# Norm rows loaded for every partition, an overflow branch moved into the last quad, and attention's last steps spread over the output projection

## The chip, the cores and the metric

The kernel runs on one core of a Trainium2 chip. The time is that of one execution on the device, in microseconds. Its engines each work through their own queue in order: TensorE (PE, weight loads as PEld), VectorE (DVE), ScalarE (ACT), GpSimd (POOL), and SyncE (SP), which here issues the loads.

## The reference

A trunk of two layers on 256 tokens of width 1024, float32. Each layer is a mixer and a mixture of experts, each followed by a norm of the sum:

```
for i in range(2):
    mix = even_mixer(x) if i == 0 else odd_mixer(x)   # SSD || stick-breaking; MLA || forgetting attention
    x = layer_norm(2**0.5 * x + mix, ln1_g[i], ln1_b[i])
    ffn = hier_moe(x)          # 4 groups x 4 experts, best group, best 2 experts of it
    x = layer_norm(2**0.5 * x + ffn, ln2_g[i], ln2_b[i])
expert e: (silu(t @ w_gate[e]) * (t @ w_up[e])) @ w_down[e], weighted by the token's gate
```

The odd mixer's eight latent-attention heads need low-rank queries (q_up) and keys and values (kv_up), a rotated key part (rope), and its eight forgetting heads a running sum of log sigmoid(f).

## The kernel before

All weights come through a ring of 19 tiles of 128 x 2048 (1 MB each). `ring_init` takes the list of loads in order; `fill` issues the next ones on SP whenever `ring_done` or `gdone` says in the program that a tile is free. SP runs in order, so a load waits until the last reader of the tile it takes is done, and everything behind it waits too. Eight loads can be under way, one per lane. Activations take tiles of the same ring (`G`), after `reserve`.

Weights of the mixers are used as sums of two rounded pieces: `split` (L230, L231) makes them, the high one on ScalarE, the low one on VectorE, `presplit` two steps ahead of TensorE.

An expert layer (`moe`) gathers up to 32 tokens for each of 16 experts, in four quads of four experts, for two halves t of the tokens. For each quad TensorE runs `gate_up` (L1054; eight weight tiles, each for both t), `act` and `turn`, the combination of the quad before, and `down` (L1084; four tiles). Results stand in PSUM: pools of four banks "a" and four "b". `overflow` is a branch in every engine's program, taken only if some expert has over 32 tokens; here it isn't. The engines do not wait for each other at it; but each waits for its own earlier work before it leaves the untaken side (L1274 EVENT_SEMAPHORE), SP for all eight lanes, and tiles that the branch uses come free when the engines that would have read them are past it. It takes all four "b" banks and stands after quad 2's `down`.

The scale and bias of a norm (1 x 2048, `ln`) are loaded into one partition of a ring tile and spread by GpSimd (`ln_rows`, L805, four broadcasts); then `gain_rows` (L812, L813) applies them to `xres`, the residual, on GpSimd. This happens in each expert layer (at quad 2), in `key_rope` of the odd mixer, and in the finale.

The odd mixer (`mixer1`) goes through a list: four value strips, q_up 0 and 1, kv_up, eight strips of q and k. On GpSimd's queue stand, in this order, `key_rope` (emitted at the first strip: clear krep, the norm's row, gain_rows of half 0, rope) and `forget` (from the second strip on). In `forget`, ScalarE takes one exponential (L200) in the middle of GpSimd's steps; in ScalarE's queue it stands ahead of the split of q_up 1's weights. Attention runs one step behind the other in `attention(j)`: scores(j), probs_T(j-1), norm_probs(j), attend(j-2). Its steps 0 to 6 go between the q and k strips, steps 7, 8, 9 after chunks 0, 1, 2 of the output projection (`out_proj`, L707 to L709, eight chunks), which uses the last head pair in chunk 7.

Of the kernel before, what the change touches and what calls it, by code (L numbers as in the profile page):

```python
# [14 lines left out]
AF = mybir.ActivationFunctionType  # L15
# [79 lines left out]
class Builder:  # L95
# [703 lines left out]
    def ln_rows(self, i):  # L799

        self.rows.add(i)
        w = self.ring[i]
        for k in range(4):
            r = w[:, 512 * k:512 * k + 512]
            self.nc.gpsimd.partition_broadcast(r, r[0:1], channels=128)  # L805
        return w.rearrange("p (k n) -> p k n", k=2)

    def gain_rows(self, t, gb, cs=slice(0, 1024)):

# [85 lines left out]
    def moe(self, layer, seq0, mixer, tiles=0):  # L895
# [303 lines left out]
        for q in (1, 2, 3):  # L1199
            if q == 2:  # L1200
                if layer == 0:
                    self.router_prep(1)
                gb = self.ln_rows(seq0 + 24)
                self.gain_rows(1, gb)
                self.gain_rows(0, gb)
            for c in range(4):
                for t in range(2):
                    gate_up(q, t, (c,))
            gate_up(q, 0, range(4, 8))
            act(q, 0)  # L1210
            if q == 1:
                rows_hi(0)
                rows_lo(0)
            gate_up(q, 1, range(4, 8))
            act(q, 1)
            turn(q, 0)
            if layer == 0 and q == 1:
                self.router_load(1)
            both(combine, q - 1, 0)
            if q == 1:  # L1220
                rows_hi(1)
                rows_lo(1)
                gather(0, 1, (1, 3))
            both(combine, q - 1, 1)
            if layer == 0 and q == 2:
                self.router_sums(1)
            turn(q, 1)
            if q == 1:
                gather(1, 1, (1, 3))
                self.gdone(2)  # L1230
            if q == 3:
                sc.preload_act_table_set(EXP_LN)
                break
            both(down, q, 0)
            if q == 2 and self.stop != "noov":
                self.reserve(2)
            both(down, q, 1)
            if q == 2 and self.stop != "noov":
                self.gdone(1)
                self.overflow(layer, [R[t]["gate"] for t in range(2)], [R[t]["ov"] for t in range(2)],  # L1240
                              n_max)
        yield
        both(down, 3, 0)
        combine(3, 0, 0)
# [19 lines left out]
    def overflow(self, layer, gate, ov, n):  # L1264

        nc = self.nc
        v, sc, pe = nc.vector, nc.scalar, nc.tensor
        gu = [self.B("fgu") for _ in range(2)]
        b, o = self.B("fht"), self.B("fo")
        fw = self.G([128, 2, 1024], name="fw")  # L1270
        fw = fw[:, 0], fw[:, 1]
        sg, ht = self.T([128, 256], name="fsg"), self.T([128, 2, 128], name="fhT")
        x1T = self.G([128, 8, 256], name="x1T")
        with self.tc.If(n > 32, label=f"over{layer}") as branch:  # L1274
            for t in range(2):

                v.scalar_tensor_tensor(ov[t], gate[t], 1.0 / ALPHA, ov[t], op0=OP.mult, op1=OP.mult)
                for c in range(8):
                    pe.transpose(b[:, :128], self.xres[:, t, 128 * c:128 * c + 128], self.ident)
                    v.tensor_copy(x1T[:, c, 128 * t:128 * t + 128], b[:, :128])  # L1280
            for e in range(16):
                q, i = divmod(e, 4)
                cs = slice(512 * i, 512 * i + 512)
                for c2 in range(4):
                    k = c2 % 2
                    nc.sync.dma_start(fw[k].rearrange("p (c n) -> p c n", c=2),
                                      self.a["wgu"][layer, q, 2 * c2:2 * c2 + 2, :, cs].rearrange("c p n -> p c n"))
                    w = fw[k].rearrange("p (c n) -> p c n", c=2)
                    for c in range(2):
                        cc = 2 * c2 + c  # L1290
                        for t in range(2):
                            pe.matmul(gu[t], x1T[:, cc, 128 * t:128 * t + 128], w[:, c, :],
                                      start=(cc == 0), stop=(cc == 7))
                for s in range(2):
                    nc.sync.dma_start(fw[s].rearrange("p (k n) -> p k n", k=2),
                                      self.a["wd"][layer, q, 2 * s:2 * s + 2, :, cs].rearrange("c p n -> p c n"))
                for t in range(2):
                    sc.activation(sg, gu[t][:, :256], AF.Silu)
                    v.tensor_mul(sg, sg, gu[t][:, 256:])
                    for k in range(2):  # L1300
                        pe.transpose(b[:, 128 * k:128 * k + 128], sg[:, 128 * k:128 * k + 128], self.ident)
                    v.tensor_copy(ht, b[:, :256].rearrange("p (k n) -> p k n", k=2))
                    for s in range(2):
                        c = slice(512 * s, 512 * s + 512)
                        for k in range(2):
                            pe.matmul(o, ht[:, k, :], fw[s][:, 512 * k:512 * k + 512], start=(k == 0), stop=(k == 1))
                        v.scalar_tensor_tensor(self.xres[:, t, c], o, ov[t][:, e:e + 1], self.xres[:, t, c],
                                               op0=OP.mult, op1=OP.add)
        if layer == 0:
            with branch.Else():  # L1310
                self.hint(1)

        self.gdone(2)
# [30 lines left out]
    def mixer1(self, s0, moe):  # L1344
# [5 lines left out]


        order = [("v", i) for i in range(4)] + [("q", 0), ("q", 1), ("kv", 0)] + [("s", i) for i in range(8)]
        first = {"v": s0 + 2, "q": s0 + 4, "kv": s0 + 5, "s": s0 + 7}

        def presplit(n):
            if n >= len(order) or order[n] in pieces:
# [87 lines left out]

        def key_rope():
            nc.gpsimd.memset(krep[:, :, :64], 0.0)
            gb.append(self.ln_rows(s0 + 6))
            for k in range(4):
                self.gain_rows(0, gb[0], slice(256 * k, 256 * k + 256))
            self.rope(nc.gpsimd, krep[:, :, 64:80], krep[:, :, 80:96], rest[:, :, 128:144], rest[:, :, 144:160],  # L1450
                      self.cv("cosk").rearrange("p (t n) -> p t n", t=2),
                      self.cv("sink").rearrange("p (t n) -> p t n", t=2), [128, 2, 16])
            nc.gpsimd.tensor_copy(krep[:, :, 96:], krep[:, :, 64:96])
# [148 lines left out]

        def attention(j):

            steps = [(scores, 0), (probs_T, 1), (norm_probs, 0), (attend, 2)]
            if j == 7:
                steps.insert(0, steps.pop())
            for f, d in steps:
                if 0 <= j - d < 8:
                    f(*divmod(j - d, 4))  # L1610

# [70 lines left out]
            m = mix[k // 4]  # L1682
            return m[:, k % 4, :], m[:, 4 + k % 4, :]

        yield from self.out_proj(8, LEAD1, wsplit, mixk, 2, 6, after=lambda k: attention(7 + k))


def moe_seq(a, layer):
# [9 lines left out]
def build(ctx, tc, a, out, stop=None):  # L1698
    b = Builder(ctx, tc, a, out, stop)
    seq = [a["w0"][i] for i in range(16)] + [a["wout0"][i] for i in range(6)]  # L1700
    m0 = len(seq)
    seq += moe_seq(a, 0)
    s1 = len(seq)
    seq += [a["wab"][0], a["wab"][1], a["wfv"][0], a["wfv"][1], a["wqu"], a["wkvu"], a["ln"][1]]
    seq += [a["wfox"][i] for i in range(4)]
    seq += [a["wout1"][i] for i in range(4)]
    m1 = len(seq)
    seq += moe_seq(a, 1) + [a["ln"][3]]
    b.ring_init(seq, {m + i for m in (m0, m1) for i in LP})
    if stop is None:  # L1710
        b.hint(0)
    nc = tc.nc
    orow = out.rearrange("(t p) d -> p t d", p=128)

    def dump_acc(gen):
        for acc in gen:
            pass
        for t in range(2):
            for s in range(2):
                nc.vector.tensor_copy(b.xres[:, t, 512 * s:512 * s + 512], acc[t][s])  # L1720
        nc.sync.dma_start(orow, b.xres)

    mix = b.mixer0()
    if stop == "mix0":
        return dump_acc(mix)
    moe = b.moe(0, m0, mix, 2)
    if stop in ("moe0", "noov"):
        return dump_acc(moe)
    mix = b.mixer1(s1, moe)
    if stop == "mix1":  # L1730
        return dump_acc(mix)
    moe = b.moe(1, m1, mix)
    next(moe)
    gb = b.ln_rows(m1 + 49)
    b.finale(gb, orow, moe)


def lay_out(inputs):
# [51 lines left out]
    wr[:, :, 8:24] = inputs["moe_w_expert"]  # L1790
    o["wr"] = f(wr.reshape(2, 8, 128, 32).transpose(0, 2, 1, 3))
    o["pp"] = pp
    o["ln"] = f(np.stack([lng, lnb], 1)).reshape(4, 1, 2048)
    gate = inputs["moe_w_gate"].reshape(2, 4, 4, 8, 128, 256)
    up = inputs["moe_w_up"].reshape(2, 4, 4, 8, 128, 256)

# [22 lines left out]
```

## Time and profile before

| what | value |
|---|---|
| median of 3 runs | 534.78 us (534.11 to 535.96) |
| profiled execution | 534.36 us, its span 532.6 us |
| granted TensorE clock, mean | 0.976 |
| data moved by DMA | 142.83 MB, mean 268 GB/s |
| GpSimd's 16 broadcasts | 12.7 us busy, 893 ns mean |

The share of the span in 40 slices of 13.3 us each (digits are tenths; 9 is 90% or more):

```profile
PE   7999999999999999999999936999999999998990
POOL 0073001120000002510000247500000002700204
PEclk9999999999999999999999986999999999999995
DMA  8999842025297799999979700460468799999602
```

TensorE is nearly always busy; the one hole in the middle (slices 24 and 25) lies in the odd mixer, and the granted clock dips behind it. DMA is full in the expert layers (slices 14 to 21 and 31 to 37) and rests around the hole.

### The profile page before, as it was taken

Reading aid. Unit: us, or ns where it says so; the run is one execution under the profiler, and the core shown is the slowest. Engines: PE = TensorE matmul, PEld = TensorE weight load, DVE = VectorE, ACT = ScalarE, POOL = GpSimd, SP = SyncE. Lnnn points to the kernel's source line nnn. Section 1 sums busy time; section 2 is a strip of 40 time slices with the busy share of each in tenths; the row PEclk is TensorE's granted clock in tenths of the full one; section 3 lists DMA queues with packets and bytes.
Section 4 is the critical chain, followed back from the end, with each engine's and each line's share of the span. In section 5 each row is a group of like instructions: output and inputs, shape, how many; then the busy total and the mean of one; then the engine's idle time right before and its main releaser. Section 6 shows DMA issues by size and latency. Waiting matters only on the chain. (4 is left out here: it accounts for less than half of the span.)

```text
span 532.6 us, 9755 instructions
## 1 busy us (share of the span) xinstructions
PE 493.0 (93%) x3859; PEld 324.6 (61%) x3859; DVE 299.2 (56%) x683; ACT 247.0 (46%) x510; POOL 83.7 (16%) x135
## 2 busy tenths in 40 slices
PE   7999999999999999999999936999999999998990
PEld 4999998898777443533335835988777443533330
DVE  5777857868877751532047705687677741512055
ACT  4686575678764341512036705566644441502041
POOL 0073001120000002510000247500000002700204
PEclk9999999999999999999999986999999999999995
DMA  8999842025297799999979700460468799999602
GB/s 339 421 420 416 325 153 80 1 79 209 61 354 282 289 397 404 422 404 423 416 290 426 313 0 1 158 225 14 159 236 322 289 418 402 422 387 422 267 1 79
DMA packets 20602, 142.83 MB, mean 268 GB/s; under 512 B 2308, under 2 KB 2564, under 8 KB 3780
## 3 DMA queue, kind: packets, MB, share of 16 engines
q1 hardware_dynamic: 19304, 136.00, 63.7%
q0 software_dynamic: 816, 5.51, 2.8%
q8 instruction: 32, 0.52, 0.4%
q10 hardware_dynamic: 432, 0.66, 0.3%
q14 instruction: 18, 0.15, 0.1%
HBM read 141.10 MB, written 1.05 MB: 267 GB/s over the span
## 5 line engine op out<-in xcount | busy, mean ns | idle before, releaser
L1054 PE MATMUL gu<-w,XT 128*32 128x512 f32 x960 | 106.2, 593 | 3.7 <-DVEq L1274 3.7
L231 DVE TENSOR_TENSOR pair<-w,pair 128x1024 fp32r<-128x1024 f32 x59 | 72.0, 1223 | 40.2 <-ACT pair L230 39.8
L1054 PEld LDWEIGHTS gu<-w,XT 128*32 128x32 f32 x960 | 31.8, 110 | 69.5 <-issue 66.7
L230 ACT ACTIVATE pair<-w 128x1024 fp32r<-128x1024 f32 x59 | 62.1, 1058 | 11.4 <-PE ps L245 6.1
L1084 PE MATMUL dn<-w,hT 128*32 128x512 f32 x512 | 57.4, 594 | 0.0
L1064 DVE TENSOR_TENSOR hd<-sg,gu 128x256 f32<-128x256 f32 x16 | 6.7, 420 | 73.9 <-ACT sg L1062 73.9
L1103 DVE SCALAR_TENSOR_TENSOR pair<-dn,ws,pair 128x512 fp32r<-128x512 f32 x30 | 22.5, 750 | 41.8 <-ACT pair L1097 39.9
L1062 ACT ACTIVATE sg<-gu 128x256 f32<-128x256 f32 x16 | 6.1, 383 | 82.6 <-PE gu L1054 82.5
L239 PE MATMUL ps<-xh,pair 128*128 128x256 f32 x288 | 42.1, 288 | 1.1 <-ACT pair L230 1.1
L242 PE MATMUL ps<-xl,pair 128*128 128x256 f32 x288 | 39.8, 280 | 0.0
L245 PE MATMUL ps<-xh,pair 128*128 128x256 f32 x288 | 39.6, 280 | 0.0
L239 PEld LDWEIGHTS ps<-xh,pair 128*128 128x128 f32 x288 | 36.4, 189 | 2.7 <-ACT pair L230 1.6
L242 PEld LDWEIGHTS ps<-xl,pair 128*128 128x128 f32 x288 | 36.5, 188 | 0.0
L245 PEld LDWEIGHTS ps<-xh,pair 128*128 128x128 f32 x288 | 36.4, 188 | 0.0
L1097 ACT ACTIVATE pair<-dn,ws 128x512 fp32r<-128x512 f32 x30 | 20.6, 687 | 33.3 <-PE dn L1084 30.6
L1084 PEld LDWEIGHTS dn<-w,hT 128*32 128x32 f32 x512 | 15.4, 110 | 33.8 <-issue 29.2
L805 POOL PARTITION_BROADCAST w<-w x16 | 12.7, 893 | 97.1 <-PE gu L1054 37.7
L1024 ACT ACTIVATE XT<-gp,pp 128x256 f32<-128x256 f32 x36 | 17.4, 562 | 18.8 <-PE gp L1017 18.8
L1565 ACT ACTIVATE pw<-z,sm 128x128 f32<-128x128 f32 (+1 forms) x32 | 13.0, 419 | 18.2 <-DVE sm L1562 12.0
L1502 PE MATMUL qu<-cthl,pair 128*128 128x256 f32 x48 | 8.7, 350 | 13.5 <-ACT pair L230 13.4
L812 POOL TENSOR_TENSOR xres<-xres,w 128x256 f32<-128x256 f32 (+1 forms) x12 | 15.3, 1279 | 32.7 <-DVE rows L1005 25.7
L303 PE MATMUL vp<-pair,xh 128*128 128x256 f32 x128 | 19.7, 288 | 0.0
(368 smaller groups left out, 928.4 us busy)
## 6 DMA issues: line engine op xcount, KB each, us to landing
w<-in_wgu_dram SPq DMA_DIRECT2D x60, 1024.0 KB, 10.5
w<-in_wd_dram SPq DMA_DIRECT2D x32, 1024.0 KB, 11.7
w<-in_w_dram SPq DMA_DIRECT2D x16, 1024.0 KB, 18.5
w<-in_wout_dram SPq DMA_DIRECT2D x10, 1024.0 KB, 17.3
wh<-in_wgu_dram POOLq DMA_DIRECT2D x4, 1024.0 KB, 9.0
w<-in_wfox_dram SPq DMA_DIRECT2D x4, 1024.0 KB, 16.3
w<-in_wfv_dram SPq DMA_DIRECT2D x2, 1024.0 KB, 5.8
w<-in_wab_dram SPq DMA_DIRECT2D x2, 848.0 KB, 18.4
```

The costliest lines, as they stand in the source:

```text
L230: self.nc.scalar.activation(vh, src, AF.Copy)
L231: (self.nc.gpsimd if pool else self.nc.vector).tensor_tensor(vl, src, vh.bitcast(F32), op=OP.subtract)
L239: mm(ps, hi[:, c, :], xh[:, c, :], start=(c == 0), stop=False)
L242: mm(ps, hi[:, c, :], xl[:, c, :], start=False, stop=False)
L245: mm(ps, lo[:, c, :], xh[:, c, :], start=False, stop=(c == n - 1))
L303: mm(o, xx[:, 4 * k + c, 128 * t:128 * t + 128], ww[:, c, :], start=(k == 0 and n == 0), stop=(k == 1 and n == 11))
L812: g.tensor_tensor(r, r, gb[:, 0, cs], op=OP.mult)
L1024: sc.activation(xt[:, c, :], b[:, i], AF.Identity, bias=bb, scale=g)
L1054: pe.matmul(gu[t][32 * e:32 * e + 32, :], XT[t][:, c, o:o + 32], w[:, e, :], start=(c == 0), stop=(c == 7))
L1084: pe.matmul(b[32 * e:32 * e + 32, :], ht[:, k, 32 * e:32 * e + 32], w[:, e, :], start=(k == 0), stop=(k == 1))
L1097: sc.activation(y, dn[t, s], AF.Copy, scale=WS[t][:, q:q + 1])
L1103: v.scalar_tensor_tensor(yl, b, WS[t][:, q:q + 1], yh.bitcast(F32), op0=OP.mult, op1=OP.subtract)
```

## The change

The rows `ln` are laid out for all 128 partitions (1 MB each) and loaded so; the broadcasts go. The odd mixer's row moves ahead of wqu and wkvu in the list of loads. `overflow` is called inside quad 3, after gate_up's first four tiles, and uses two "b" banks in place of four (its body then works on one half of the tokens at a time). Attention's steps 7, 8, 9 follow chunks 0, 2, 4 of the output projection, and in 8 and 9, as in 7 before, attend comes first.

```
     def ln_rows(self, i):
         self.rows.add(i)
-        w = self.ring[i]
-        for k in range(4):
-            r = w[:, 512 * k:512 * k + 512]
-            self.nc.gpsimd.partition_broadcast(r, r[0:1], channels=128)
-        return w.rearrange("p (k n) -> p k n", k=2)
+        return self.ring[i].rearrange("p (k n) -> p k n", k=2)
...
             for c in range(4):
                 for t in range(2):
                     gate_up(q, t, (c,))
+            if q == 3 and self.stop != "noov":
+                self.gdone(1)
+                self.overflow(layer, ...)
             gate_up(q, 0, range(4, 8))
...
             both(down, q, 1)
-            if q == 2 and self.stop != "noov":
-                self.gdone(1)
-                self.overflow(layer, ...)
...
-        gu = [self.B("fgu") for _ in range(2)]
-        b, o = self.B("fht"), self.B("fo")
+        gu, b = self.B("fgu"), self.B("fht")
...
-            steps = [(scores, 0), (probs_T, 1), (norm_probs, 0), (attend, 2)]
-            if j == 7:
-                steps.insert(0, steps.pop())
-            for f, d in steps:
+            for f, d in ((scores, 0), (probs_T, 1), (norm_probs, 0), (attend, 2)) if j < 7 else (
+                    (attend, 2), (scores, 0), (probs_T, 1), (norm_probs, 0)):
...
-        yield from self.out_proj(8, LEAD1, wsplit, mixk, 2, 6, after=lambda k: attention(7 + k))
+        steps = {0: 7, 2: 8, 4: 9}
+        yield from self.out_proj(8, LEAD1, wsplit, mixk, 2, 6, after=lambda k: k in steps and attention(steps[k]))
...
-    seq += [a["wab"][0], a["wab"][1], a["wfv"][0], a["wfv"][1], a["wqu"], a["wkvu"], a["ln"][1]]
+    seq += [a["wab"][0], a["wab"][1], a["wfv"][0], a["wfv"][1], a["ln"][1], a["wqu"], a["wkvu"]]
...
-    o["ln"] = f(np.stack([lng, lnb], 1)).reshape(4, 1, 2048)
+    o["ln"] = f(np.broadcast_to(np.stack([lng, lnb], 1).reshape(4, 1, 2048), (4, 128, 2048)))
```

How it moves instructions, at three places. GpSimd at key_rope, before (w is the ring tile with the norm's row, krep the key's rotated part; each broadcast is an ISA row, and the bare ISA rows set GpSimd's configuration):

```order
L1446 MEMSET krep 128x2x64
L805 ISA
L805 ISA w<-w 128x512 x4
L812 ISA
L812 TENSOR_TENSOR xres<-xres,w 128x256
```

and now (the numbers of lines are those of the changed kernel):

```order
L1437 MEMSET krep 128x2x64
L808 TENSOR_TENSOR xres<-xres,w 128x256
L809 TENSOR_TENSOR xres<-xres,w 128x256
L808 TENSOR_TENSOR xres<-xres,w 128x256
L809 TENSOR_TENSOR xres<-xres,w 128x256
```

The gains follow the memset directly. TensorE at the branch of layer 0, before (fht and fgu belong to the branch's body):

```order
L1071 MATMUL ht<-cc,hd 128x128 x2
L1084 MATMUL dn<-w,hT 32x512 x32
L1274 COMPARE_AND_BRANCH
L1279 MATMUL fht<-cc,xres 128x128 x16
L1292 MATMUL fgu<-fw,x1T 128x512 x16
```

and now:

```order
L1067 MATMUL ht<-cc,hd 128x128 x2
L1080 MATMUL dn<-w,hT 32x512 x32
L1050 MATMUL gu<-w,XT 32x512 x32
L1270 COMPARE_AND_BRANCH
L1275 MATMUL fht<-cc,xres 128x128 x16
```

Half of quad 3's shared gate_up stands ahead of it. SP at the same place, before (fw is the body's own weight tile):

```order
L173 DMA w<-in_wgu_dram 128x2048 x8
L173 DMA w<-in_wd_dram 128x2048 x4
L173 DMA w<-in_wab_dram 128x1696 x2
L1274 COMPARE_AND_BRANCH
L1286 DMA fw<-in_wgu_dram 128x2x512 x4
```

and now:

```order
L173 DMA w<-in_wab_dram 128x1696 x2
L173 DMA w<-in_wfv_dram 128x2048 x2
L173 DMA w<-in_ln_dram 128x2048
L173 DMA w<-in_wqu_dram 128x2048
L1270 COMPARE_AND_BRANCH
```

Four more loads of the odd mixer stand ahead of the branch, the row of the norm among them. ScalarE in the output projection, before (pu are transposed probabilities, mixf the result of attend, pair and wb pieces of the output weights):

```order
L1587 ACTIVATE pu<-pT 128x384
L230 ACTIVATE pair<-w 128x1024
L1587 ACTIVATE pu<-pT 128x384
L1600 ACTIVATE mixf<-ao 128x256
L230 ACTIVATE wb<-w 128x1024
L1600 ACTIVATE mixf<-ao 128x256
L230 ACTIVATE wb<-w 128x1024 x3
```

and now:

```order
L1578 ACTIVATE pu<-pT 128x384
L230 ACTIVATE pair<-w 128x1024
L230 ACTIVATE wb<-w 128x1024
L1591 ACTIVATE mixf<-ao 128x256
L1578 ACTIVATE pu<-pT 128x384
L230 ACTIVATE wb<-w 128x1024 x2
L1591 ACTIVATE mixf<-ao 128x256
L230 ACTIVATE wb<-w 128x1024
```

One split moves ahead of the last probs_T, and two more ahead of the last attend.

More of the change, by code (lines that the diff above doesn't have):

```diff
@@ L1208, in moe @@
                     gate_up(q, t, (c,))
+            if q == 3 and self.stop != "noov":
+                self.gdone(1)
+                self.overflow(layer, [R[t]["gate"] for t in range(2)], [R[t]["ov"] for t in range(2)],
+                              n_max)
             gate_up(q, 0, range(4, 8))
@@ L1237, in moe @@
             both(down, q, 1)
-            if q == 2 and self.stop != "noov":
-                self.gdone(1)
-                self.overflow(layer, [R[t]["gate"] for t in range(2)], [R[t]["ov"] for t in range(2)],
-                              n_max)
         yield
@@ L1280, in overflow @@
                     v.tensor_copy(x1T[:, c, 128 * t:128 * t + 128], b[:, :128])
-            for e in range(16):
+            for e, t in ((e, t) for e in range(16) for t in range(2)):
                 q, i = divmod(e, 4)
@@ L1284, in overflow @@
                 for c2 in range(4):
[L1285 to L1288, printed above, removed]
+                    w = fw[c2 % 2].rearrange("p (c n) -> p c n", c=2)
+                    nc.sync.dma_start(w, self.a["wgu"][layer, q, 2 * c2:2 * c2 + 2, :, cs].rearrange("c p n -> p c n"))
                     for c in range(2):
                         cc = 2 * c2 + c
-                        for t in range(2):
-                            pe.matmul(gu[t], x1T[:, cc, 128 * t:128 * t + 128], w[:, c, :],
-                                      start=(cc == 0), stop=(cc == 7))
+                        pe.matmul(gu, x1T[:, cc, 128 * t:128 * t + 128], w[:, c, :], start=(cc == 0), stop=(cc == 7))
                 for s in range(2):
@@ L1296, in overflow @@
                                       self.a["wd"][layer, q, 2 * s:2 * s + 2, :, cs].rearrange("c p n -> p c n"))
-                for t in range(2):
-                    sc.activation(sg, gu[t][:, :256], AF.Silu)
-                    v.tensor_mul(sg, sg, gu[t][:, 256:])
-                    for k in range(2):
[L1301 to L1308, printed above, removed]
+                sc.activation(sg, gu[:, :256], AF.Silu)
+                v.tensor_mul(sg, sg, gu[:, 256:])
+                for k in range(2):
+                    pe.transpose(b[:, 128 * k:128 * k + 128], sg[:, 128 * k:128 * k + 128], self.ident)
+                v.tensor_copy(ht, b[:, :256].rearrange("p (k n) -> p k n", k=2))
+                for s in range(2):
+                    c = slice(512 * s, 512 * s + 512)
+                    for k in range(2):
+                        pe.matmul(b, ht[:, k, :], fw[s][:, 512 * k:512 * k + 512], start=(k == 0), stop=(k == 1))
+                    v.scalar_tensor_tensor(self.xres[:, t, c], b, ov[t][:, e:e + 1], self.xres[:, t, c],
+                                           op0=OP.mult, op1=OP.add)
         if layer == 0:
@@ L1352, in mixer1 @@
         order = [("v", i) for i in range(4)] + [("q", 0), ("q", 1), ("kv", 0)] + [("s", i) for i in range(8)]
-        first = {"v": s0 + 2, "q": s0 + 4, "kv": s0 + 5, "s": s0 + 7}
+        first = {"v": s0 + 2, "q": s0 + 5, "kv": s0 + 6, "s": s0 + 7}
         def presplit(n):
@@ L1446, in key_rope @@
             nc.gpsimd.memset(krep[:, :, :64], 0.0)
-            gb.append(self.ln_rows(s0 + 6))
+            gb.append(self.ln_rows(s0 + 4))
             for k in range(4):
```

## The prediction

> **What bounds the kernel now.** I read the busy shares first, then TensorE's waits, then the timeline around the longest one.
>
> ```profile
> PE 493.0 (93%) x3859; PEld 324.6 (61%) x3859; DVE 299.2 (56%) x683; ACT 247.0 (46%) x510; POOL 83.7 (16%) x135
> PE qu L1502 <- ACT pair L230: 13.4, 1, 13.4
> PE gu L1054 <- DVEq L1274: 3.7, 2, 1.9
> PE pT L1582 <- DVE pw L1574: 1.0, 1, 1.0
> ```
>
> TensorE is busy for 493 of 532.6 us, so time is won only where it waits. The waits (engine, line, releaser: total, times, longest) that the change can touch are these three: 13.4 us once at q_up, 3.7 us at the two overflow branches, 1.0 us in attention's last steps. No DMA stands among the releasers of its long waits. The 13.4 us, in order of time (start, duration, engine; in brackets the idle time before):
>
> ```profile
> 293.39 0.20 POOL L1446 MEMSET krep<- 128x128 f32 x1 [64.67 <-DMA w<-in_wout_dram]
> 303.12 4.31 POOL L805 PARTITION_BROADCAST w<-w  x4 [9.53 <-PE ct L1482]
> 308.02 2.98 PE L1502 MATMUL qu<-cthl,pair 128*128 128x256 f32 x24
> 314.40 0.71 POOL L812 TENSOR_TENSOR xres<-xres,w 128x256 f32<-128x256 f32 x1 [6.96 <-issue]
> 322.94 0.22 POOL L198 TENSOR_TENSOR sptmp<-sptmp,fz 128x16 f32<-128x16 f32 x1
> 323.20 0.21 ACT L200 ACTIVATE sptmp<-sptmp 128x16 f32<-128x16 f32 x1 [18.35 <-POOL sptmp L198]
> 323.32 1.04 ACT L230 ACTIVATE pair<-w 128x1024 fp32r<-128x1024 f32 x1
> 324.41 5.73 PE L1502 MATMUL qu<-cthl,pair 128*128 128x256 f32 x24 [13.42 <-ACT pair L230]
> 329.98 1.57 PE L1514 MATMUL ku<-cthl,pair 128*128 128x256 f32 x12
> L805 POOLq MODIFY_POOL_CONFIG  x2: 11/11/11, 293.8 to 293.8; - x2
> ```
>
> TensorE lacks q1's weights; ScalarE cannot split them because its queue stands behind one small exponential (L200); that one waits for GpSimd, which is late because of the broadcast. GpSimd is set to another configuration at 293.8, starts broadcasting only 9.3 us later, at 303.12, ends at 307.43, and starts its next ordinary operation 7.0 us after that, at 314.40. So spreading one row costs 314.40 - 293.8 = 20.6 us of the chain, of which 4.3 us are broadcasts. The stall also lowers the clock (columns: PE busy, ..., granted clock, DMA share, GB/s):
>
> ```profile
> 305.00:310.00 5.00, 5.00 (x44) 5.00 (x43) 1.11 (x1) 0.00 (x0) 2.44 (x3) 1.00 0.00 0
> 315.00:320.00 5.00, 0.00 (x0) 0.00 (x0) 0.00 (x0) 0.00 (x0) 4.68 (x8) 0.61 0.00 0
> 325.00:330.00 5.00, 4.96 (x24) 4.67 (x24) 4.47 (x7) 2.22 (x3) 3.58 (x7) 0.52 0.00 0
> ```
>
> After some 5 us without TensorE work the clock is granted at about half, and the same 24 matmuls that took 2.98 us at 308.02 take 5.73 us at 324.41.
>
> **Part 1, the rows of the norms.** Removed: 16 broadcasts and their configuration switches. Three of the four groups were off the path (in the two expert layers and the finale GpSimd then waits for its operands anyway). At key_rope GpSimd goes from the memset (end 293.59) straight to L812, so L198 and L200 come up to 20.6 us earlier, at about 302.4 us. ScalarE is then ready for q1's split before TensorE ends q0 at 311.0. Nothing else holds q1: TensorE goes on at 311.0, needs 2.9 us, and reaches L1514 at 313.9 where it was 329.98: **-16.1 us** (13.4 wait, 2.7 clock). What is late next would be kv's split, but ScalarE stood idle for 18.35 us up to L200 and has the time.
>
> The Trainium skill (GPSIMD Engine Reference, section 2.1 Instruction dispatch) says that the first call to a freshly loaded GpSimd library pays about 6 us of code loading that no instruction shows. The trace has 9.3 and 7.0 us for the two switches, somewhat more. By the page's figure the same broadcast would end 3.3 us sooner and the whole step 4.3 us sooner, and removing it would win that much less; the measured rows decide.
>
> Added: each row is now 1 MB in place of 8 KB, so 4 MB more on SP's queue. At the full rate that is 2.5 us each:
>
> ```profile
> 260.00:265.00 5.00, 5.00 (x52) 1.82 (x48) 0.00 (x0) 0.25 (x1) 0.00 (x0) 1.00 1.00 414
> 265.00:270.00 5.00, 5.00 (x42) 2.50 (x35) 0.84 (x2) 0.90 (x3) 0.00 (x0) 1.00 0.52 217
> 270.50 3.64 PE L1084 MATMUL dn<-w,hT 128*32 128x512 f32 x32
> 500.00:505.00 5.00, 5.00 (x52) 1.68 (x44) 0.42 (x1) 0.38 (x1) 2.57 (x4) 1.00 0.22 93
> 507.67 3.64 PE L1084 MATMUL dn<-w,hT 128*32 128x512 f32 x32
> w<-in_wab_dram SPq DMA_DIRECT2D x2, 848.0 KB, 18.4
> w<-in_wqu_dram SPq DMA_DIRECT2D x1, 1024.0 KB, 10.0
> ```
>
> The load stream of layer 0's experts runs dry at 265 + 0.52 x 5 = 267.6; the last two loads in it are wab (2 x 848 KB, 4.1 us), so the last expert tile is in at about 263.5, 7 us before the down projection of quad 3 starts at 270.50. In layer 1 it runs dry at 501.1, 6.6 us before 507.67. The added megabyte takes 2.5 us of that, the branch (below) about 1.5 more; 2.6 us are left in the tighter place. I cost the bytes at **0**; if that cover is gone, each us of it is one us of TensorE. The rows at key_rope are loaded before wqu, and DMA rests from 305 on; wqu is not late before, so this row isn't either. The finale needs its row only after 519.
>
> **Part 2, the branch inside quad 3.** Before, it stands between quad 2's down projection and quad 3's first gate_up, and holds all four banks of the pool "b", the last freed by VectorE:
>
> ```profile
> 221.91 7.07 PE L1084 MATMUL dn<-w,hT 128*32 128x512 f32 x64
> 228.80 1.47 PE L1054 MATMUL gu<-w,XT 128*32 128x512 f32 x12
> 245.27 7.07 PE L1084 MATMUL dn<-w,hT 128*32 128x512 f32 x64
> 253.13 0.75 DVE L1103 SCALAR_TENSOR_TENSOR pair<-dn,ws,pair 128x512 fp32r<-128x512 f32 x1 [0.96 <-ACTq L1274]
> 254.19 12.22 PE L1054 MATMUL gu<-w,XT 128*32 128x512 f32 x112 [1.85 <-DVEq L1274]
> L1274 PEldq EVENT_SEMAPHORE  x1: 51/51/51, 252.4 to 252.4; - x1
> L1274 SPq COMPARE_BRANCH  x1: 70/70/70, 251.1 to 251.1; - x1
> L1274 SPq EVENT_SEMAPHORE  x8: 17/17/17, 263.2 to 270.0; - x8
> 270.10 0.84 SPq L173 DMA_DIRECT2D w<-in_wfv_dram  x2
> ```
>
> From quad 1 to 2, with no branch, gate_up starts 6.89 us after the down projection's start; from 2 to 3 it is 8.92: the branch costs 2.03 us in each layer. Now TensorE goes into quad 3 at once, and VectorE is past its last eviction (253.88) long before TensorE comes to the branch after 16 groups. It still has to drain there: its own semaphore of the untaken side came 0.07 us after the last matmul's end. How long TensorE then takes to go on is hidden by the wait for VectorE; bounds: nothing, and the 1.85 us of the old wait. SP, the nearest row, issued its next load 0.1 us after its last semaphore (270.0, next DMA at 270.1). I take 0.5 us for drain and jump, as a matmul's last 0.16 us no longer overlaps. 2 x (2.03 - 0.5) = **-3.1 us** (ends: -4.1 and -0.4).
> SP's wait at the branch (263.2 to 270.0: eight semaphores, one per DMA lane, each for what is still under way) moves behind wfv, the row and wqu, 4 MB or 10 us later, to about 282. Behind it are wkvu, wfox, wout and the next layer's experts; wkvu, the first, lands by 292 even if it takes the 10 us that wqu took from issue to landing, and TensorE needs it at 313.9. So that is 0.
>
> **Part 3, attention's last steps.** probs_T(7) now comes a chunk later and behind attend(6), so the 0.97 us wait goes; ScalarE's splits of wout move ahead of it. The wait's row stands above; the transposes behind it were stretched as well. Ends: 0 and -1.6; I take **-1.2**. If the last split came late, chunk 7 would wait; its split follows attend(7) with some 2.8 us of chunks in between, for about 2.3 us of ScalarE and VectorE work.
>
> **What comes against it.** The eight gain operations (L812, L813; eight of 0.71, 5.7 us) now run at 293.6 to 300, not in the stall but beside VectorE's splits:
>
> ```profile
> 296.98 1.22 DVE L231 TENSOR_TENSOR pair<-w,pair 128x1024 fp32r<-128x1024 f32 x1
> 297.76 0.64 PE L303 MATMUL vp<-pair,xl 128*128 128x256 f32 x4
> 521.03 0.75 DVE L822 SCALAR_TENSOR_TENSOR xres<-xres,mv,w 128x512 f32<-128x512 f32 x1
> 522.86 1.71 POOL L831 TENSOR_TENSOR xres<-xres,w 128x512 f32<-128x512 f32 x1
> 523.37 1.75 DVE L822 SCALAR_TENSOR_TENSOR xres<-xres,mv,w 128x512 f32<-128x512 f32 x1
> 331.28 1.23 DVE L231 TENSOR_TENSOR pair<-w,pair 128x1024 fp32r<-128x1024 f32 x1 [0.22 <-ACT pair L230]
> 331.32 1.30 POOL L208 TENSOR_SCALAR sptmp<-sptmp 128x16 f32<-128x16 f32 x1
> ```
>
> In the finale VectorE's 0.75 us became 1.75 where GpSimd had begun first; at 331 a GpSimd operation of 16 columns took 1.30 us, about as long as the split that VectorE had begun. Whoever is second waits. From 293.4 up to and with the split at 296.98 some seven VectorE operations could each wait for up to one gain operation (0.72 us), half on average: 2.5 us. TensorE's need of the xl half at 297.76 leaves about 1.3. Ends 0 and 3.5; I take **+1.2**.
> The Trainium skill (SBUF — State Buffer, section Who interferes with whom) calls the pair of ports that VectorE and GpSimd share an exclusive lock, taken for the whole instruction when VectorE reads two SBUF inputs; these rows agree, and by it the +1.2 is real and may be the whole 3.5.
>
> **The sum.** -16.1 - 3.1 - 1.2 + 1.2 + 0 = -19.2. The profiled execution took 534.36, 0.4 below the median of 534.78; from the two it is 515.2 and 515.6. I forecast **515.5 us**.
>
> **Rivals.**
> a) The shared port costs the full 3.5 us: 518. For it: the rows at 523 and 331. Against: VectorE has short operations on one tensor there, too.
> b) GpSimd stays late for another reason than the configuration. For it: the broadcast's start at 303.12 falls on the end of the load stream (DMA 0.00 from 305). Then only broadcast and second switch go, 11.3 us; L200 comes at 311.9, q1's split at 313.0, TensorE waits 2.1 us with no slow clock: 517.6. Against: the second gap of 7 us has no DMA at all.
> c) The other side: SP is held in the branch. It must now get slots for four more loads first, and nothing behind passes until eight lanes are empty. If wqu's slot came free only with the last tile of quad 3, SP would leave at about 300, wfox would land near 310, and it costs nothing yet; it decides from the point where wfox's first tile lands after 315, and the kernel is slower only if that is after 334 (19 us of wait). For it: SP waited 19 us in the branch before (251 to 270). Against: by the order SP's extra loads follow gate_up's first tiles.
> d) Expert tiles come late: the 2.6 us of cover are gone and each layer waits 1 to 3 us: 517 to 521.
> e) The change moves nothing that matters, since another wait takes q1's place: 530 to 535.
>
> **How the numbers follow.** The sum as it stands 0.55 (513.0 to 517), a) 0.17, b) 0.08, d) 0.10, e) 0.05, c) 0.05. A difference under 0.3% (1.6 us) cannot be told from none by this measurement. The range takes the likeliest with its low end (no contention, branch at its better end) and a), b), d): **512.8 to 521**, about 0.85. Faster 0.94, same 0.02, slower 0.04.
>
> **What would show it.** Right: no TensorE wait at q_up over 1 us and no granted clock of 0.5 between 300 and 320; no GpSimd broadcast; gate_up of quad 3 about 6.9 us after quad 2's down projection; no wait at pT. Gains beside splits longer than 0.72 and 1.22 us show the port; a wait of gu or dn for a DMA shows d). Wrong: L200 later than 311, or a new TensorE wait for wkvu or wfox.

## The result and the profile after

The changed kernel takes **512.42 us** (median of 4 runs, 511.98 to 512.64); the kernel before took 534.49 in its 4 runs (534.11 to 535.96). The ratio is 0.958 (0.956 to 0.960). The forecast was 515.5 (512.8 to 521), 3.1 us above the result, whose value lies 0.4 us under the range. The profiled execution after took 511.98 us, its span 510.2, so 22.4 us less span than before.

The busy shares and slices of the changed kernel's page (TensorE busy 96% of the span):

```profile
PE 490.4 (96%) x3859; PEld 321.4 (63%) x3859; DVE 300.8 (59%) x683; ACT 246.8 (48%) x510; POOL 75.5 (15%) x119
...
PE   6999999999999999999999999999999999999990
...
POOL 0074000120000000070000187300000000610004
PEclk9999999999999999999999999999999999999996
```

The hole in slices 24 and 25 is gone, and with it the dip of the granted clock. Of the three waits only a rest stands in TensorE's list; q_up and pT are not in it. The second row is new, a matmul at a value strip that waits for VectorE's split:

```profile
PE gu L1050 <- PEq L1270: 0.4, 2, 0.2
...
PE vp L303 <- DVE pair L231: 0.3, 1, 0.3
```

The chain at key_rope in order of time:

```profile
291.62 0.20 POOL L1437 MEMSET krep<- 128x128 f32 x1 [63.07 <-ACT junk L1384]
291.80 0.73 POOL L808 TENSOR_TENSOR xres<-xres,w 128x256 f32<-128x256 f32 x1
303.28 1.21 POOL L198 TENSOR_TENSOR sptmp<-sptmp,fz 128x16 f32<-128x16 f32 x1
305.34 0.20 ACT L200 ACTIVATE sptmp<-sptmp 128x16 f32<-128x16 f32 x1
307.53 5.80 PE L1493 MATMUL qu<-cthl,pair 128*128 128x256 f32 x48
```

and the windows around q_up (columns as before: PE busy, ..., granted clock, DMA share, GB/s):

```profile
305.00:310.00 5.00, 5.00 (x45) 5.00 (x43) 3.28 (x5) 3.51 (x6) 2.79 (x6) 1.00 0.11 44
310.00:315.00 5.00, 5.00 (x44) 4.99 (x43) 4.60 (x7) 2.68 (x4) 4.15 (x11) 1.00 0.01 3
```

GpSimd goes from the memset straight into the gains; the small exponential (L200) runs at 305.34 instead of 323.20, and the 48 matmuls of q_up run in one piece of 5.80 us at full clock. L200 still comes 2.9 us later than the 302.4 of the forecast: beside VectorE's splits GpSimd's own operations got longer too (the last gain 1.59 us where 0.72 is usual, L198 1.21 where it took 0.22). Nothing had to wait for it.

Since TensorE runs the same 3859 matmuls in both kernels, in another order only around the output projection, the two traces can be set against each other matmul by matmul. How far the changed kernel is ahead at eight landmarks (starts, but for the last two) gives each step's gain without any sum of waits:

| landmark | before | after | ahead | step (forecast) |
|---|---|---|---|---|
| first `down` matmul of quad 2, layer 0 | 245.27 | 245.17 | 0.1 | |
| first `down` matmul of quad 3, layer 0 | 270.50 | 268.74 | 1.8 | branch: 1.7 (1.5) |
| first q_up matmul | 308.02 | 307.53 | 0.5 | gains beside splits: -1.3 (-1.2) |
| first matmul of kv_up | 329.98 | 313.17 | 16.8 | wait and slow clock: 16.3 (16.1) |
| last matmul of the output projection | 409.27 | 391.05 | 18.2 | attention's steps: 1.4 (1.2) |
| first `down` matmul of quad 3, layer 1 | 507.67 | 487.79 | 19.9 | branch: 1.7 (1.5) |
| end of VectorE's last operation | 526.78 | 506.86 | 19.9 | 0 |
| end of the span | 532.6 | 510.2 | 22.4 | **2.4 (not in the forecast)** |

Up to VectorE's last operation the steps come out within 0.2 us each: 19.8 us against the 19.2 forecast. The other 2.4 us (unrounded, the last two leads are 19.92 and 22.36) come behind VectorE's last operation, where the prediction had looked at nothing. VectorE's last operation starts at 525.15 before and at 505.23 after, and takes 1.63 us in both. The rows of the closing sequence behind it (instructions of one line: count, durations in ns least/median/most, first to last start), before:

```profile
L1815 POOLq DRAIN  x3: 52/109/2285, 524.6 to 529.9; - x3
L1815 POOLq EVENT_SEMAPHORE  x4: 17/17/17, 529.3 to 532.5; - x4
```

and after:

```profile
L1805 POOLq DRAIN  x3: 40/109/2285, 504.7 to 509.9; - x3
L1805 POOLq EVENT_SEMAPHORE  x4: 17/17/17, 509.4 to 510.1; - x4
```

Before, GpSimd starts its last drain at 529.9 (52 ns) and its last semaphore at 532.5, 2.6 us after the drain's start; after, at 509.9 and 510.1, 0.2 us later. All other engines wait for it there. The DMA queues of the kernel before between 530 and 532 us held one packet, of the kind "instruction":

```profile
DMA packets 1, 0.01 MB, mean 4 GB/s; under 512 B 0, under 2 KB 0, under 8 KB 0
## 3 DMA queue, kind: packets, MB, share of 16 engines
q14 instruction: 1, 0.01, 1.2%
```

After, the last 1.2 us of the span hold none. So the experiments had two tasks: to see whether each part does alone what the landmarks say, and to find out what the 2.4 us are.

### The profile page after: what moved, and what is told of

Its sections match the earlier page's. It is cut to its first block, busy times and chain, and to the rows that moved or that the text cites. A ratio compares the mean times of both kernels' runs of the same rounds, so it can differ in the third digit from the quotient of the medians.

```text
span 510.2 us, 9714 instructions
## 1 busy us (share of the span) xinstructions
PE 490.4 (96%) x3859; PEld 321.4 (63%) x3859; DVE 300.8 (59%) x683; ACT 246.8 (48%) x510; POOL 75.5 (15%) x119
## 5 line engine op out<-in xcount | busy, mean ns | idle before, releaser
L231 DVE TENSOR_TENSOR pair<-w,pair 128x1024 fp32r<-128x1024 f32 x59 | 72.4, 1231 | 23.0 <-ACT pair L230 22.4
L303 PE MATMUL vp<-pair,xh 128*128 128x256 f32 x128 | 19.8, 290 | 0.3 <-DVE pair L231 0.3
L408 DVE SCALAR_TENSOR_TENSOR cy<-ps,pp,cy 128x255 f32<-128x255 f32 (+2 forms) x36 | 17.3, 480 | 2.0 <-ACT cy L405 1.1
L162 POOL DMA_DIRECT2D wh<-in_wgu_dram x4 | 2.2, 555 | 108.5 <-PE acc L709 108.5
## 6 DMA issues: line engine op xcount, KB each, us to landing
w<-in_wd_dram SPq DMA_DIRECT2D x32, 1024.0 KB, 13.6
```

The source lines that it names most:

```text
L231: (self.nc.gpsimd if pool else self.nc.vector).tensor_tensor(vl, src, vh.bitcast(F32), op=OP.subtract)
L303: mm(o, xx[:, 4 * k + c, 128 * t:128 * t + 128], ww[:, c, :], start=(k == 0 and n == 0), stop=(k == 1 and n == 11))
L408: v.scalar_tensor_tensor(y[:, k:], ps[:, :256 - k], self.pp[:, i:i + 1], y[:, k:], op0=OP.mult, op1=OP.add)
```

## Experiments

The times before are 534.6 to 534.7 us (medians of 9 to 21 runs) in the comparisons below.

### Each part alone, and the bytes alone

On the kernel before: part 1 (ln_rows without broadcasts, rows of 1 MB, the odd mixer's row ahead of wqu); part 2 (the diff of `overflow` and `moe`); part 3 (the diff of `attention` and its steps); and the rows' layout alone, with GpSimd still spreading partition 0:

```
-    o["ln"] = f(np.stack([lng, lnb], 1)).reshape(4, 1, 2048)
+    o["ln"] = f(np.broadcast_to(np.stack([lng, lnb], 1).reshape(4, 1, 2048), (4, 128, 2048)))
```

> Part 1 alone on the kernel before: rows of the norms loaded for all partitions, no broadcasts, branch and attention as before. By the ledger of the two traces (q_up's wait and slow clock -16.2, VectorE's splits beside the gains +1.1, the end of the program after the last output 2.5 us shorter): 17.6 us less than before, 516.9. By the prediction's account, in which the end of the program is not touched: -16.1 + 1.2 = 14.9 us less, 519.6. The two are told apart by the time from VectorE's last operation to the end of the span: 5.8 us before, 3.3 by the ledger.

> Part 2 alone: the overflow branch inside quad 3 on two banks. Ledger: -1.8 in layer 0 and -1.5 in layer 1, 3.3 us less, 531.2; what is left of the branch on TensorE is some 0.2 to 0.4 us each. Prediction's account: 0.5 us left in each, 3.1 less. Rival (the gain of layer 0 is lost again, because q_up's wait is set by GpSimd's chain and not by TensorE): only layer 1's 1.5 us, 533.0. The end of the program stays at 5.8 us, since the broadcasts are still there.

> Part 3 alone: attention's last steps after chunks 0, 2 and 4. Ledger: 1.5 us less, 533.0, with the wait at pT gone. Prediction's account: 1.2 less. Rival (the time at the second layer's start is set by something behind TensorE): no change, 534.5.

> The bytes of part 1 alone: the rows are loaded for all partitions (1 MB each), but GpSimd still spreads partition 0 over them, in the old order of loads. If the 4 MB are hidden, as they were costed: within 0.5 us of before, 534.5, no TensorE wait on a DMA. If the cover is too thin (rival d of the prediction): 1 to 3 us more in each expert layer, 536.5 to 540.

| run | time | ratio (interval) | steps by the landmarks |
|---|---|---|---|
| part 1 | 517.39 | 0.967 (0.966 to 0.968) | strips -1.3, q_up 16.3, closing 2.4 |
| part 2 | 532.49 | 0.996 (0.994 to 0.997) | branches 1.7 and 1.7, q_up to attention -0.9 |
| part 3 | 533.83 | 0.998 (0.997 to 0.999) | attention's end 1.4, q_up and behind -0.6 |
| bytes | 535.03 | 1.001 (1.000 to 1.002) | q_up and behind -0.4, closing -0.2, else 0 |

Part 1 alone gives 17.2 us by the medians and 17.6 by the ratio: the 17.6 of the ledger (the table of landmarks), not 14.9. From VectorE's last operation to the end of the span its trace has 3.3 us, those of parts 2 and 3 and of the bytes 5.9 to 6.0, the kernel before 5.8. The bytes cost nothing that can be told from none, and no new TensorE wait for a DMA appears: rival d is out. Parts 2 and 3 bring their steps in the landmarks (1.7 twice, 1.4), but only 2.1 and 0.8 us of time. Two things vary between executions here. The start does: one matmul of the first mixer stands at 15.34 us before and 15.32 after, but at 15.97 to 16.04 in the traces of the three parts. And where the stop at key_rope is still there, its length does: with part 2 alone q_up 1 starts 17.0 us after q_up 0, before 16.4. GpSimd's way back from the broadcasts took 7.6 us in that trace, before 7.0. The rival that GpSimd's chain keeps its place and swallows the gain of layer 0 is not borne out, since its memset comes 1.1 us sooner (292.33 for 293.39), as q_up 0 does. By the ratios the parts bring 17.6, 2.4 and 1.1 us, in sum 21.1, and all together 22.4, each with 0.5 to 1.1 us to both sides; that they add up to less than the whole isn't shown.

### What the last 2.4 us are

Two theories: A, GpSimd has to fetch its next instructions there, and where that falls depends on how many it has behind it; B, the broadcasts' own code has taken the place of something that the end needs. The changed kernel got small memsets on GpSimd in `ln_rows`, or the finale's broadcasts back (N stands for the number of memsets in one call):

```
     def ln_rows(self, i):
         self.rows.add(i)
+        pad = self.S([128, 8], name="pad", bufs=1)
+        for k in range(N):          # in sum 26, 7 (in the finale only), 34
+            self.nc.gpsimd.memset(pad, 0.0)
```

> The changed kernel with 26 small memsets on GpSimd (6 to 8 where each of the four groups of broadcasts was), so that its program is as long as before in every stretch; no broadcast. Theory A (GpSimd stands at the end of the program because its next instructions have to be fetched there, and where that falls depends on the length of its program): from VectorE's last operation to the end of the span 5.8 us again, with an 8 KB instruction fetch in it, 2.5 us more than the changed kernel, 514.9. Theory B (the stop is due to the broadcasts' own code having taken the place of other code): 3.3 us as in the changed kernel, 512.4.

> The changed kernel with 7 small memsets on GpSimd in the finale alone. Theory A: 5.8 us at the end only if those 7 instructions alone move the place of the fetch into the end (counted from the last branch), else 3.3. Theory B: 3.3 us, 512.4.

> The changed kernel with the four broadcasts of the finale alone put back (on rows that are loaded in full): as many GpSimd instructions as in the run with 7 memsets in the finale. Theory A: the same end as that run. Theory B: 5.8 us at the end, 514.9. In both the finale before VectorE's last operation stays as it is, since GpSimd waits some 15 us there (the prediction's cost of 0 for this group).

> The changed kernel with 34 small memsets in place of the 16 broadcasts and 18 changes of configuration that GpSimd executed before, 8 more than in the run with 26, so that it executes as many instructions as before. Theory A (the place of an instruction fetch): the fetch, which with 26 memsets came 2.2 us after the last recorded instruction, falls back inside the span: 5.8 us from VectorE's last operation to the end, and the time again 514.6. Theory B (the broadcasts' own code): 3.3 us and 512.4.

| run | GpSimd instructions in the trace | time | span | time less span |
|---|---|---|---|---|
| before | 196 | 534.49 (534.11 to 535.96) | 532.6 | 1.8 |
| after | 162 | 512.42 (511.98 to 512.64) | 510.2 | 1.8 |
| 7 memsets in the finale | 169 | 512.83 (512.23 to 513.53) | 510.4 | 1.8 |
| broadcasts of the finale back | 171 | 512.59 (512.09 to 512.80) | 510.7 | 1.8 |
| 26 memsets | 188 | 514.68 (514.62 to 514.76) | 510.6 | 4.0 |
| 34 memsets | 196 | 515.13 (514.82 and 515.45) | 513.0 | 1.8 |

(Times are medians with the lowest and highest run. Spans are of the profiled execution, and the last column is that execution's own time less its span.) With 34 memsets and not one broadcast the stop is back in its old place: GpSimd's closing semaphores, and the DMA between 510.5 and 512.9 us:

```profile
L1808 POOLq DRAIN  x3: 46/109/2288, 505.0 to 510.3; - x3
...
L1808 POOLq EVENT_SEMAPHORE  x4: 17/17/17, 509.8 to 512.9; - x4
...
q14 instruction: 1, 0.01, 1.1%
```

With 26 the span ends as in the changed kernel, but the time is 2.3 us longer by the medians, and one instruction packet comes behind the last recorded instruction (window 511 to 514 of a span that ends at 510.6):

```profile
L1808 POOLq EVENT_SEMAPHORE  x4: 17/17/17, 509.8 to 510.5; - x4
...
q14 instruction: 1, 0.01, 1.0%
```

For 26 memsets I had expected the longer span, and there the place of the stop was missed by 8 instructions; the time, 514.68 against 514.9, was not. Theory B is out: the finale's broadcasts bring nothing back, and 34 memsets bring everything. So of the 22 us, 2.4 have nothing to do with norms. They come from 34 GpSimd instructions less in the program. Two more signs bear this out. Of all the traces here, five have the stop (before, parts 2 and 3, the bytes, 34 memsets), and in each an instruction packet lies in it; in the other nine no packet lies inside the closing sequence. And with part 2 alone, where GpSimd has 197 instructions, one more than before, the stop stands one instruction earlier, in front of the last drain (527.97 to 530.41) and not behind it. That the packet carries GpSimd's instructions is inferred from its place in GpSimd's stop; the trace does not name whose it is.

The Trainium skill (Runtime: NRT & Kernel Launch, section Instruction fetch mechanics) says that each sequencer fetches its next block of instructions while it executes the current one, at a cost that is "mostly hidden". If the packet is GpSimd's, these runs show a place where it isn't hidden: 2.2 to 2.4 us at the very end.

### The stop at key_rope, put back into the changed kernel

Once with all four broadcasts (L805 of before, in key_rope only), and once with a single small one:

```
+            r = self.ring[s0 + 4][:, :64]
+            nc.gpsimd.partition_broadcast(r, r[0:1], channels=128)
```

> The changed kernel with the four broadcasts put back in key_rope alone (on a row that is loaded in full). If the prediction's account of this stop is right (20.6 us on GpSimd's chain, wherever the rest of the kernel stands): a TensorE wait of some 13.4 us at q_up, slow clock behind it for 2.7, and the 1.1 us of collisions at the value strips gone: 15.1 us more than the changed kernel, 527.5. Rival (part of it was the place of the row in the order of loads, or the branch): less than 12 us more.

> The changed kernel with one small broadcast (64 columns) in key_rope, in place of four of 512. If the price is the change of GpSimd's configuration, there and back, and not the broadcasts' work: some 16 of the 20.6 us stay, q_up waits about 10 us, 524 us. If the price goes with the data that is spread: 512.4 to 514.

Measured: 527.70 us (ratio 0.987, 0.985 to 0.988) and 526.06 (0.984, 0.982 to 0.985). GpSimd with one small broadcast, in order of time:

```profile
291.61 0.20 POOL L1437 MEMSET krep<- 128x128 f32 x1 [63.09 <-ACT junk L1384]
301.22 0.80 POOL L1440 PARTITION_BROADCAST w<-w  x1 [9.40 <-PE ct L1475]
311.14 0.71 POOL L808 TENSOR_TENSOR xres<-xres,w 128x256 f32<-128x256 f32 x1 [9.12 <-issue]
```

and with four:

```profile
302.41 4.00 POOL L806 PARTITION_BROADCAST w<-w  x4 [10.01 <-DVE pair L231]
313.42 0.71 POOL L813 TENSOR_TENSOR xres<-xres,w 128x256 f32<-128x256 f32 x1 [7.01 <-issue]
```

TensorE waits at q_up for 11.9 us with one and 13.7 with four. The four cost 15.3 us, as expected (15.1), on a kernel in which everything else is changed. One broadcast of 0.80 us costs 13.6: between the memset's end and the first gain lie 19.3 us, of which 18.5 are the two changes of configuration (9.4 and 9.1). It costs more than the 12 us expected, because the change back took 9.1 us, where the traces with four broadcasts have 7.0 to 7.6; why is not shown. The price is there and back, not the work between. The figure of the Trainium skill (GPSIMD Engine Reference, section 2.1 Instruction dispatch: about 6 us for the first call to a freshly loaded library, in no instruction) is exceeded on both ways there, 9.4 and 10.0 us; for the way back, 9.1 and 7.0 us here, that section states none.

### What the branch still costs

The changed kernel without `overflow` in both layers (which leaves out tokens beyond 32 for one expert; this input has none).

> The changed kernel without the overflow branch, in both layers (tokens over 32 for one expert would be left out; in this input no expert has so many). It gives what the branch still costs. Ledger: 0.2 us of TensorE idle each and as much of lost overlap, 0.4 to 0.8 us less in all, 511.6 to 512.0. Prediction's account: 0.5 us each, 1.0 less, 511.4. Rival (SP's wait for its eight lanes costs something later): more than 1.5 us less.

Measured: 511.15 us (ratio to before 0.956, 0.954 to 0.957), 1.3 less than the changed kernel's median, with runs of either kernel 0.7 apart. By the landmarks each branch step becomes 2.1 us in place of 1.7, so 0.4 us remain of each branch, half of it the wait, the rest the overlap of matmuls that it breaks: without the branch the next matmul starts 0.18 us before the end of the one ahead of it. Of the 1.3 us the two branches so account for 0.8; the other 0.5 is not explained by the traces, and lies within the spread of the runs. TensorE in the changed kernel, where the branch lies between the two `gu` rows, and SP's first load behind its own wait:

```profile
245.17 7.07 PE L1080 MATMUL dn<-w,hT 128*32 128x512 f32 x64
252.06 7.05 PE L1050 MATMUL gu<-w,XT 128*32 128x512 f32 x64
259.29 1.06 PE L1050 MATMUL gu<-w,XT 128*32 128x512 f32 x8 [0.18 <-PEq L1270]
280.33 0.34 SPq L173 DMA_DIRECT2D w<-in_wkvu_dram  x1
```

### The gains out of the way

```
         def key_rope():
-            for k in range(4):
-                self.gain_rows(0, gb[0], slice(256 * k, 256 * k + 256))
...
-                if i < 2:
-                    for k in (2 * i, 2 * i + 1):
-                        self.gain_rows(1, gb[0], slice(256 * k, 256 * k + 256))
+                if i < 4:
+                    for k in (2 * (i % 2), 2 * (i % 2) + 1):
+                        self.gain_rows(i // 2, gb[0], slice(256 * k, 256 * k + 256))
```

> The changed kernel with the eight gain operations of half 0 moved from key_rope behind the first q and k strips, in front of those of half 1, so that VectorE's splits of the value strips have the port for themselves. By the ledger (three short TensorE waits of 1.1 us in all at the value strips): 1.1 us less, 511.3, and the splits there back at 1.22 us. By the prediction's wide end 3.5 us less, 508.9. Rival (the gains collide as much with VectorE's splits of the strips): no change, 512.4.

Measured: 512.06 us (ratio to before 0.958, 0.957 to 0.960), 0.4 less than the changed kernel and not to be told from it. The changed kernel at the value strips in order of time (VectorE, the last gain, the matmul that waits), and a normalisation of attention:

```profile
292.61 0.74 DVE L218 TENSOR_TENSOR mt<-ss 128x2 f32<-128x2 f32 x1 [0.57 <-ACT ss L1389]
295.55 1.82 DVE L1375 TENSOR_TENSOR xl<-xu,xh 128x512 fp32r<-128x512 f32 x2
297.29 1.75 DVE L231 TENSOR_TENSOR pair<-w,pair 128x1024 fp32r<-128x1024 f32 x1
298.03 1.59 POOL L809 TENSOR_TENSOR xres<-xres,w 128x256 f32<-128x256 f32 x1
299.09 1.22 PE L303 MATMUL vp<-pair,xh 128*128 128x256 f32 x8 [0.31 <-DVE pair L231]
323.82 0.28 DVE L1565 TENSOR_SCALAR pw<-pw,sm 128x128 f32<-128x128 f32 x1
```

The same split and the same normalisation with the gains moved, and the gain that now runs beside the latter:

```profile
295.52 1.22 DVE L231 TENSOR_TENSOR pair<-w,pair 128x1024 fp32r<-128x1024 f32 x1
322.75 0.85 POOL L809 TENSOR_TENSOR xres<-xres,w 128x256 f32<-128x256 f32 x1
322.94 0.75 DVE L1563 TENSOR_SCALAR pw<-pw,sm 128x128 f32<-128x128 f32 x1
```

The split is back at 1.22 us and the 1.3 us at the value strips are won in full: by the landmarks the step there is 0. But half 1's gains now run 4.4 us later, beside attention's normalisation (0.75 us where it takes 0.28 without a gain beside it), and between kv_up and the output projection 0.8 us are lost, 0.7 of them in front of one transposition of probabilities (pT). The collision was moved, and 0.8 of its 1.3 us came back.

## Why the prediction was right and where it fell short

- **Part 1** (-16.1): 16.3. The whole chain holds, from configuration to slow clock, shown by taking it out of the kernel before and by putting it back into the changed one. Rival b (GpSimd late for another reason) is out. The 4 MB of bytes cost 0, as costed: the load stream of layer 1, with the row as its last load, rests from 486.2 (0.23 of the window below), and TensorE starts the last quad's `down` at 487.79 without a wait. That leaves a cover of 1.6 us, where the prediction had 2.6.

```profile
485.00:490.00 5.00, 5.00 (x40) 2.60 (x40) 0.42 (x1) 2.66 (x5) 0.00 (x0) 1.00 0.23 92
```

- **Part 2** (-3.1): 3.3. The rest of each branch is 0.4 us where I took 0.5. gate_up follows `down` at 6.89 us, as forecast. SP leaves the branch at 280.33 where I had 282, and nothing waits for it: rival c is out.
- **Part 3** (-1.2): 1.4, nearer to its end of 1.6, with no wait at pT.
- **The port** (+1.2): 1.3. The gains did hold up VectorE (1.75 for 1.22, 0.74 for 0.16), most of it without a wait that the list shows; rival a's 3.5 was too much: from the memset's start to the end of the split VectorE takes 7.4 us where it took 4.8, so 2.6 us more, about the 2.5 of the prediction, and TensorE loses half of that. The Trainium skill's exclusive lock (SBUF — State Buffer, section Who interferes with whom) agrees with these rows, but says nothing of how much of it reaches TensorE.
- **The step that failed** is "Three of the four groups were off the path (in the two expert layers and the finale GpSimd then waits for its operands anyway)". That is true of the broadcasts' time, and I stopped there. With "time is won only where it waits", said of TensorE, the prediction took the stretch behind VectorE's last operation, 5.8 us in the trace before, as fixed. It isn't. It held 2.6 us between the starts of two neighbouring GpSimd instructions, with an instruction packet in between, and it depends on how many instructions GpSimd has. With that term, worth 2.4 us, the sum would have been -21.6, or 512.8 to 513.2 by the two bases. The low end of the range was built from the known terms alone, and so the result fell under it: no bound had been given to the closing sequence. The other 0.6 us are the first three terms above, each 0.2 to 0.3 better than taken, less the port's 0.1.

## What to carry to other kernels

Price a custom GpSimd operation by the switch there and back (16 to 19 us here), not by its own time, and ask what stands behind it on the queue; three of four such places were free here, and the fourth cost 15 to 16 us. Set two traces against each other by the same matmuls: a ledger by landmarks splits a gain into its steps better than sums of waits do. And read the end of the trace behind the last useful operation as well: removing instructions can move a stop out of the measured time, and a gain that comes from there isn't owed to the idea that was tried.

## What was not expected of the hardware

- A stop of GpSimd at the end, in all likelihood an instruction fetch, cost 2.2 to 2.4 us, and with 188 instructions it lay outside the recorded span but inside the measured time (4.0 us between the two in place of 1.8).
- At key_rope the change of GpSimd's configuration took 8.7 to 10.0 us to the first broadcast, and 7.0 to 7.6 us back after four broadcasts but 9.1 after one.
- VectorE operations of two columns waited for GpSimd as whole splits did: 0.74 in place of 0.16 us.
- A branch that isn't taken cost TensorE 0.4 us where nothing else had to be waited for.
